# The second product of two feed-forwards: from plain products half by half to seven block products for both halves

## The chip, the cores and the metric

The kernel runs on one core of one Trainium2 chip. The metric is the device time of one execution in microseconds (us), as the median of several runs; a run with a profile leaves one execution in detail. Engines are named as in the profile: PE is TensorE (matmul), PEld its weight loads, DVE is VectorE, ACT is ScalarE, POOL is GpSimd, SP is SyncE, which here does nothing but issue all the DMAs, in one queue and in order.

## The reference

One layer of a trunk with 1,024 prompt tokens and 64 sample tokens (8 sequences of 8), a model width of 1,024 and a feed-forward width of 2,816, all in float32:

```python
def rmsnorm(x, g):
    y = x * lax.rsqrt(jnp.mean(x * x, axis=-1, keepdims=True) + EPS)
    return y * g

def swiglu(x, w_in, w_out):
    gu = x @ w_in                                  # 1024 -> 2 * 2816
    g, u = gu[..., :D_FF], gu[..., D_FF:]
    return (jax.nn.silu(g) * u) @ w_out            # 2816 -> 1024

x = x + 0.5 * swiglu(rmsnorm(x, norm_ffn1), ffn1_w_in, ffn1_w_out)
x = x + token_mixing(rmsnorm(x, norm_mix), ...)    # projections, pooling, convolution, scan, gates
x = x + 0.5 * swiglu(rmsnorm(x, norm_ffn2), ffn2_w_in, ffn2_w_out)
y = rmsnorm(x, norm_final)
```

The change lies in `(silu(g) * u) @ w_out`, the second product of each of the two feed-forwards, and in what stands next to it.

## The kernel before

**Tokens.** They lie in two halves: h0 has 512 (all prompt), h1 has 576 (512 prompt, 64 sample). Activations are kept transposed, features on the 128 partitions and tokens along the row, so a tile of h1 is 128x576. The width of 1,024 makes 8 blocks of rows (m or k), the feed-forward width 22 (ff).

**Products in float32.** An operand is split into a rounded part and the rest of it (names `hh` and `hr`, `wh` and `wl`, `hi` and `lo`, or both in one tile, `hl` and `hp`): ACT writes the rounded part, DVE subtracts it (`split`, L356 and L358; for weights L295 and L296 in `load_w`). A block product is then three matmuls: rounded by rounded, rounded weight by the rest, rest of the weight by rounded. All matmuls have one line, L164, and all transposes L168; they are told apart by the tile they write (`po` is the second product's).

**The stages.** Feed-forward 1, the projections into the token mixing (`in_proj`), the mixing, feed-forward 2, the final norm. In a feed-forward the first product is already done by seven block products instead of eight (`wino`, `ffn_in`), one ff after the other, with sums of weight blocks on GpSimd (L438) and parts of its exits on GpSimd too (L554, L575, L605). The gated hidden tile `g` of one ff and half goes to DRAM: `dma(hdram[h][ff], g)`.

**The second product before** (`ffn`, from L665 on) runs half by half. For a half all 22 hidden tiles are loaded (`hr<-hd`) and split; then for each of the 8 blocks of output rows, over 22 blocks of the inner dimension, `products` issues three matmuls of 512 columns for h0, or three times two matmuls of 288 columns for h1. That is 528 matmuls of 512 columns and 1,056 of 288 in each feed-forward. The weights of output blocks 0 and 1 were split ahead and wait in DRAM (`part`, `out01`); those of the others are loaded raw and split at the place. Each block leaves through DVE (L697: half the product plus the old x, which is reloaded from `xspill`).

**Order.** The program is written with generators ("chains") that are advanced at every step of a product (`tick()`), due at times of a count of matmul time: `start(gen, delay)` sets one going, `finish` runs it to its end. A scheduler then fixes an order for each engine, and every engine works through its own list in order. After feed-forward 1, `after1` starts the norm of the next stage as such a chain: for h0 it runs 25 us of that count into h1's second product (`HN_AT`), its normalised tiles go through DRAM (`xnd`) and come back. h1's norm follows h1's last block. In feed-forward 2 `half2` and `after2` do the same with the final norm, whose first part (`final_head`, output rows 0 to 3) and second part (`final`) transpose x and write the result.

## Time and profile before

| | before |
|---|---|
| runs | 2918.49 us median of 3 (2917.91 to 2923.22) |
| profiled execution | 2918.88 us, its span 2917.1 us |
| mean granted PE clock | 0.988 |
| PE, DVE, ACT, POOL busy | 97%, 58%, 47%, 34% |
| second product of feed-forward 1 | 523.4 to 788.7 us |
| second product of feed-forward 2 | 2633.9 to 2903.0 us |

The span is what the profile's records cover. The profile is one execution; "busy" of PE counts matmuls whose ends are modelled, and since matmuls are pipelined, the time of one in a group's row (from its start to its result) is longer than the distance between two. In a group's row stand line, engine, operation, tile written and tile read, the count, then the busy time in us, the mean of one in ns, and the idle time of the engine just before it with what ended it.

### The profile page before, as it was taken

How to read it: one execution, taken by the hardware profiler on the slowest of the kernel's cores; microseconds unless marked ns; L12 is line 12 of the kernel's file. 1: busy time of each engine (PE TensorE's matmuls, PEld its weight loads, DVE VectorE, ACT ScalarE, POOL GpSimd, SP SyncE). 2: the span in 40 equal slices, each digit the busy share in tenths (PEclk: the TensorE clock that was granted, in tenths of full speed). 3: DMA queues.
4: the chain of work that ended last, by engine and by line, in shares of the span. 5: the costliest groups of instructions: out<-in, count | busy, mean ns of one | idle time of the engine just before them, and what ended most of it. 6: DMA issues, size and time to landing. Idle time of an engine off the chain costs nothing. (4 is left out here: it accounts for less than half of the span.)

```text
span 2917.1 us, 52535 instructions
## 1 busy us (share of the span) xinstructions
PE 2828.8 (97%) x19306; PEld 2614.7 (90%) x19306; DVE 1706.4 (58%) x2702; ACT 1364.7 (47%) x3004; POOL 999.3 (34%) x1088
## 2 busy tenths in 40 slices
PE   7999999999999999999989999899999999999998
PEld 6999999889989999999988887678999999997898
DVE  6665555434483586766757776765665544453422
ACT  5444444323354555554556566566234444442322
POOL 6444444000132456464712343322134444440000
PEclk9999999999999999999999999998999999999999
DMA  4575554856445555634375678775764522236642
GB/s 134 168 226 183 162 173 130 283 185 194 115 129 164 163 188 162 201 107 128 104 263 182 198 230 247 251 252 171 251 230 144 163 92 82 78 118 200 218 156 73
DMA packets 520802, 502.84 MB, mean 172 GB/s; under 512 B 36564, under 2 KB 365128, under 8 KB 520536
## 3 DMA queue, kind: packets, MB, share of 16 engines
q1 hardware_dynamic: 520528, 499.47, 54.0%
q8 instruction: 152, 2.49, 0.4%
q14 instruction: 106, 0.87, 0.1%
q10 hardware_dynamic: 16, 0.00, 0.0%
HBM read 356.53 MB, written 143.05 MB: 171 GB/s over the span
## 5 line engine op out<-in xcount | busy, mean ns | idle before, releaser
L164 PE MATMUL pw<-X,wh 128*128 128x288 f32 (+2 forms) x2832 | 626.7, 310 | 3.8 <-ACT v L561 3.6
L164 PEld LDWEIGHTS pw<-X,wh 128*128 128x128 f32 x2832 | 461.7, 189 | 25.7 <-ACT v L561 4.2
L164 PE MATMUL pw<-X,wl 128*128 128x288 f32 (+1 forms) x1644 | 473.6, 288 | 0.6 <-DVE wl L445 0.6
L164 PE MATMUL pw<-hl,wh 128*128 128x256 f32 (+1 forms) x1536 | 393.1, 329 | 0.0
L445 DVE TENSOR_TENSOR wl<-s,wh 128x512 fp32r<-128x512 f32 x288 | 227.2, 790 | 238.3 <-ACT wh L444 216.4
L164 PE MATMUL pw<-hi,wh 128*128 128x288 f32 x1120 | 331.1, 296 | 1.1 <-ACT t L597 1.1
L164 PE MATMUL pw<-hi,wl 128*128 128x288 f32 x1120 | 329.8, 294 | 0.0
L164 PE MATMUL pw<-lo,wh 128*128 128x288 f32 x1120 | 329.7, 294 | 0.0
L438 POOL TENSOR_TENSOR s<-wraw,wraw 128x512 f32<-128x512 f32 x144 | 195.8, 1360 | 357.5 <-DVE wl L445 253.9
L164 PEld LDWEIGHTS pw<-X,wl 128*128 128x128 f32 x1644 | 311.7, 190 | 0.8 <-DVE wl L445 0.8
L164 PE MATMUL pw<-hl,wl 128*128 128x256 f32 x1072 | 300.7, 281 | 0.0
L296 DVE TENSOR_TENSOR wl<-wraw,wh 128x512 fp32r<-128x512 f32 x208 | 151.3, 729 | 246.6 <-ACT wh L295 241.5
L164 PEld LDWEIGHTS pw<-hl,wh 128*128 128x128 f32 x1536 | 259.8, 190 | 20.9
L295 ACT ACTIVATE wh<-wraw 128x512 fp32r<-128x512 f32 x208 | 125.6, 605 | 310.8 <-PE po L164 213.7
L444 ACT ACTIVATE wh<-s 128x512 fp32r<-128x512 f32 x288 | 181.1, 630 | 162.6 <-PE pw L164 138.3
L445 DVE TENSOR_TENSOR wl<-wraw,wh 128x512 fp32r<-128x512 f32 x216 | 168.7, 781 | 135.3 <-ACT wh L444 124.7
L164 PEld LDWEIGHTS pw<-hi,wh 128*128 128x128 f32 x1120 | 210.5, 188 | 7.8 <-ACT t L597 1.6
L164 PE MATMUL po<-hh,wh 128*128 128x288 f32 (+1 forms) x800 | 211.2, 324 | 4.4 <-ACT hh L356 3.5
L164 PE MATMUL po<-hr,wh 128*128 128x288 f32 (+1 forms) x800 | 211.6, 323 | 0.1
L164 PE MATMUL po<-hh,wl 128*128 128x288 f32 (+1 forms) x800 | 210.9, 323 | 0.0
L164 PEld LDWEIGHTS pw<-lo,wh 128*128 128x128 f32 x1120 | 210.6, 188 | 0.0
L164 PEld LDWEIGHTS pw<-hi,wl 128*128 128x128 f32 x1120 | 210.1, 188 | 0.0
(380 smaller groups left out, 6252.7 us busy)
## 6 DMA issues: line engine op xcount, KB each, us to landing
wraw<-in_ffn_w_in_dram SPq DMA_DIRECT2D x188, 256.0 KB
wh<-part SPq DMA_DIRECT2D x156, 256.0 KB
wl<-part SPq DMA_DIRECT2D x156, 256.0 KB
wraw<-in_w_in_dram SPq DMA_DIRECT2D x144, 256.0 KB
wraw<-in_ffn_w_out_dram SPq DMA_DIRECT2D x120, 256.0 KB
part<-ph SPq DMA_DIRECT2D x80, 256.0 KB
part<-pr SPq DMA_DIRECT2D x80, 256.0 KB
ab<-acsd SPq DMA_DIRECT2D x64, 256.0 KB
```

Source lines behind the costliest of these rows:

```text
L164: T.matmul(out, lhsT, rhs, start=start, stop=stop, skip_group_check=free)
L295: S.activation(wh, raw, AF.Copy)
L296: V.tensor_tensor(wl, raw, wh.bitcast(F32), op=ALU.subtract)
L438: G.tensor_tensor(t, a, b, op=op)
L444: S.activation(wh, a, AF.Copy)
L445: V.tensor_tensor(wl, a, wh.bitcast(F32), op=ALU.subtract)
```

## The change

The second product of both feed-forwards becomes `second`: 7 block products in place of 8 over a 2x2x2 cut (ff tiles even and odd; output rows 0 to 3 and 4 to 7; the first and second half of each token half), in the order 1, 2, 5, 6, 4, 7, 3. Each product runs over 4 output blocks and 11 pairs of ff tiles, with three matmuls of 256 columns (h0) and three of 288 (h1) beside each other on the same weights: 7 x 4 x 11 x 3 = 924 pairs in each feed-forward.

Its operands on the token side are seven sets of 11 tiles of 128x544, made in the first product's stage and put to DRAM (`hblock`): three are quarters of the hidden tiles (products 1, 2, 3), four are sums that GpSimd makes in place by a chain (`sums`, four subtractions for each half and pair of ff tiles). On the weight side nothing is split ahead any more: products 1, 2 and 4 take one raw weight block, 5, 6 and 7 a sum of GpSimd's, 3 what `fourth` left during product 4. Results are combined at the exits (`leave`). The last product is done for both halves on output rows 0 and 1, then for h0 on rows 2 and 3, then for h1, so that h0 ends 66 matmuls of 288 columns ahead of h1. h0's norm no longer runs beside h1's second product, and the round trip through `xnd` is gone; a part of the sum of squares is made ahead (`half1`), as are half of the stores of x.

```diff
-    def rstd(tiles, h, count, out, pace=1.0):
+    def rstd(tiles, h, count, out, pace=1.0, s=None):
...
-                dma(hdram[0][ff], g[:, : 2 * n])
+                hidden(0, ff, g)
...
-        for h in HALVES:
-            N = NTOK[h]
-            parts = [], []
-            for k in range(NFF):
...
-                dma(t, hdram[h][k])
-                split(t, a[:, :N], t.bitcast(F32R))
...
-            for ms in ((0, 1),) + tuple((m,) for m in range(2, KD)):
...
-                        wh, wl = load_w(wo, kb, n4, m * P)
-                        for kk in range(n4):
-                            products([pts], wh, wl, kk, slice(0, P), [(h, *parts)], kb + kk, NFF)
...
-            after(h, xt)
+        while hsums:
+            finish(hsums.pop(0))
+        second(wo, after, half)
...
+    def hidden(h, ff, g):
...
+        if ff % 2 == 0:
+            even[h] = g
+            put("1", g[:, f])
+            return
+        e = even[h]
+        put("2", g[:, f])
+        put("3", g[:, s_])
+
+        def sums():
+            for p, out, a, b in (("5", e[:, s_], e[:, s_], e[:, f]), ("6", g[:, s_], g[:, s_], e[:, s_]),
+                                 ("7", e[:, f], g[:, s_], e[:, f]), ("4", g[:, f], g[:, f], g[:, s_])):
+                G.tensor_tensor(out, a, b, op=ALU.subtract)
+                put(p, out)
+                yield H_PACE
+
+        hsums.append(start(sums(), H_AT))
...
+        def load_X(p):
...
+            dma(r, hblock[p][k])
+            split(r, a, r.bitcast(F32R))
...
+        def unit(p, m, hs, ws):
+            pts = [psum("pd", "po" + p)[:, : NPAIR[h]] for h in hs]
+            for kb, nk, wh, wl in ws:
+                for kk in range(nk):
...
+                    for j, (W_, lo_) in enumerate(((wh, 0), (wh, 1), (wl, 0))):
+                        for h, pt in zip(hs, pts):
...
+                            mm(pt, W_[:, kk, :], X[p][k][lo_][:, at : at + NPAIR[h]],
...
+            for h, pt in zip(hs, pts):
+                leave(p, m, h, pt)
...
+            for m in range(4):
...
+                unit(p, m, HALVES, weights(p, m))
+                if p == "4":
+                    fourth(m)
+                for _ in range((0, 3, 3, 2)[m]):
+                    load_X(nxt)
+        for h in HALVES:
+            half(h, xt[h])
+        for m in (0, 1):
+            unit("3", m, HALVES, weights("3", m))
...
+        for h in HALVES:
+            for m in (2, 3):
+                unit("3", m, [h], kept[m] if h else keep(m))
+            after(h, xt[h])
...
     def after1(h, xt):
         o = []
-        if h == 0:
-            prep1m[0] = start(norm_parts(xt, 0, i_gm, o, HN_PACE, xnd), HN_AT), o
-        for m in range(KD):
+        s, c = ssq1[h]
+        finish(c)
+        prep1m[h] = start(norm_parts(xt, h, i_gm, o, (0.5, 1.2)[h], s), 0.0), o
+        for m in range(4):
             dma(xspill[h][m], xt[m][:, : NTOK[h]])
-        if h == 1:
-            finish(prep1m[0][0])
...
-            for k in (0, 4, 1, 5, 2, 6, 3, 7):
-                dma(xn[k][:, : NTOK[0]], xnd[k])
...
-    ffn(wi1, ffn1_w_out[0], prep1, after1, side=side())
+    ffn(wi1, ffn1_w_out[0], prep1, after1, half1, side())
```

Three places of the order that the change gives, each before and after. In the rows stand the line, the operation, the tile written and the tiles read with their numbers, the shape, and in brackets the engines and queues whose signals the instruction waits for.

PE where feed-forward 1 ends and `in_proj` begins, before: `po` is the second product, `pdt` the first result of the projections, and `hl` are the normalised tiles of h0, one number for each of the 8 blocks.

```order
L164 MATMUL po_8616<-hh_7331,wl_8769 128x288
L164 MATMUL pdt_8813<-hl_7838,wh_8815 128x512 [waits Activation_49]
L164 MATMUL pdt_8813<-hl_7838,wh_8815 128x512
L164 MATMUL pdt_8813<-hl_7838,wl_8816 128x512 [waits DVE_49]
L164 MATMUL pdt_8813<-hl_7868,wh_8815 128x512 x2
L164 MATMUL pdt_8813<-hl_7868,wl_8816 128x512
L164 MATMUL pdt_8813<-hl_7904,wh_8815 128x512 x2
```

The same place after; `pg` is the result of the gates' projection.

```order
L165 MATMUL po_1646_9454<-hh_9102,wl_9382 128x288
L165 MATMUL pdt_9540<-hl_9501,wh_9542 128x512 [waits Activation_49]
L165 MATMUL pg_1681_9605<-hl_9501,wh_9607 128x512
L165 MATMUL pdt_9540<-hl_9501,wh_9542 128x512 [waits DVE_49]
L165 MATMUL pdt_9540<-hl_9501,wl_9543 128x512
L165 MATMUL pdt_9540<-hl_9506,wh_9542 128x512 [waits Activation_49]
L165 MATMUL pg_1681_9605<-hl_9501,wh_9607 128x512
L165 MATMUL pg_1681_9605<-hl_9501,wl_9608 128x512
L165 MATMUL pg_1681_9605<-hl_9506,wh_9607 128x512
L165 MATMUL pdt_9540<-hl_9506,wh_9542 128x512 [waits DVE_49]
```

Before, `pdt` waited for the weights' two parts alone, and the tiles `hl` stood ready; now each block's `hl` is itself waited for, its rounded part from ACT and its rest from DVE, and the gates' matmuls are put between.

DVE around h0's norm, before: `xn` is the normalised tile, `hl` its rest, `wl` the rest of a weight tile of h1's second product, `x` an exit of it.

```order
L393 TENSOR_SCALAR rsm_7761<-pss_7756 128x4 [waits PE_49]
L296 TENSOR_TENSOR wl_7857<-wraw_7855,wh_7856 128x256 [waits DMAHW2_49,PE_49,Activation_49]
L799 SCALAR_TENSOR_TENSOR xn_7837<-x_6575,cols,r_7800 128x512 [waits Activation_49]
L296 TENSOR_TENSOR wl_7887<-wraw_7885,wh_7886 128x512 [waits DMAHW3_49,PE_49,Activation_49]
L358 TENSOR_TENSOR hl_7838<-xn_7837,hl_7838 128x512 [waits Activation_49]
L799 SCALAR_TENSOR_TENSOR xn_7867<-x_6578,cols,r_7800 128x512 [waits DMAHW3_49,DVE_49]
L296 TENSOR_TENSOR wl_7923<-wraw_7921,wh_7922 128x512 [waits DMAHW4_49,PE_49,Activation_49]
L358 TENSOR_TENSOR hl_7868<-xn_7867,hl_7868 128x512 [waits Activation_49]
L697 SCALAR_TENSOR_TENSOR x_7879<-po_7682,x_7879 128x288 [waits PE_49]
```

The same after; L795 is an exit of the last product, L946 what was L799.

```order
L397 TENSOR_SCALAR rsm_9447<-pss_9442 128x4 [waits PE_49]
L795 SCALAR_TENSOR_TENSOR x_7148<-po_1639_9399,x_7148 128x288 [waits PE_49]
L296 TENSOR_TENSOR wl_9608<-wraw_9606,wh_9607 128x512 [waits DMAHW1_49,Activation_49]
L946 SCALAR_TENSOR_TENSOR xn_9500<-x_6954,cols,r_9479 128x512 [waits Activation_49]
L795 SCALAR_TENSOR_TENSOR x_7252<-po_1646_9454,x_7252 128x288 [waits PE_49,Pool_49]
L946 SCALAR_TENSOR_TENSOR xn_9505<-x_7044,cols,r_9479 128x512
L358 TENSOR_TENSOR hl_9501<-xn_9500,hl_9501 128x512 [waits Activation_49]
L946 SCALAR_TENSOR_TENSOR xn_9510<-x_7146,cols,r_9479 128x512
L358 TENSOR_TENSOR hl_9506<-xn_9505,hl_9506 128x512 [waits Activation_49]
L946 SCALAR_TENSOR_TENSOR xn_9515<-x_7250,cols,r_9479 128x512
```

Before, the norm's steps were spread between the weights of h1's long second product; now the first of them stands just ahead of the last exit of the whole second product (`x_7252`), and the others follow it.

POOL in the first product's stage of feed-forward 1, before, one ff: L438 are sums of weight blocks for the next ff, the others the exits.

```order
L438 TENSOR_TENSOR s_741_3939<-wraw_3869,wraw_3871 128x512 [waits DMAHW1_49,DMAHW0_49,DVE_49]
L438 TENSOR_TENSOR s_742_3941<-s_741_3939,wraw_3865 128x512 [waits DMAHW5_49,DVE_49,Pool_49]
L554 TENSOR_TENSOR g_3639<-g_3639 128x256 [waits DVE_49]
L438 TENSOR_TENSOR s_754_4004<-wraw_3865,wraw_3869 128x512 [waits DVE_49]
L438 TENSOR_TENSOR s_758_4035<-wraw_3867,s_742_3941 128x512 [waits DMAHW4_49,DVE_49,Pool_49]
L554 TENSOR_TENSOR t_3640<-t_3640 128x256 [waits DMAHW2_49,DVE_49]
L554 TENSOR_TENSOR g_3639<-v_3641 128x256 [waits DVE_49,Pool_49]
```

A piece of the same stage after, in which one pair's sums stand (L702):

```order
L579 TENSOR_TENSOR g_4757<-g_4757,t_4758 128x256 [waits Activation_49]
L609 TENSOR_TENSOR g_4775<-g_4775,t_4774 128x288 [waits Activation_49]
L702 TENSOR_TENSOR g_4757<-g_4757,g_4503 128x256 [waits DMAHW3_49,Pool_49]
L702 TENSOR_TENSOR g_4503<-g_4757,g_4503 128x256 [waits DMAHW4_49,Pool_49]
L442 TENSOR_TENSOR s_941_5270<-wraw_5202,wraw_5204 128x512 [waits DMAHW2_49,DMAHW1_49,DVE_49]
L702 TENSOR_TENSOR g_4775<-g_4775,g_4521 128x288 [waits DMAHW5_49]
L702 TENSOR_TENSOR g_4757<-g_4757 128x256 [waits DMAHW6_49]
L702 TENSOR_TENSOR g_4521<-g_4775,g_4521 128x288 [waits Pool_49]
L702 TENSOR_TENSOR g_4775<-g_4775 128x288 [waits DMAHW0_49]
L442 TENSOR_TENSOR s_942_5272<-s_941_5270,wraw_5198 128x512 [waits DVE_49]
```

The subtractions stand in POOL's list between the exits and the weight sums, and most of them wait for a DMA queue: they write over a tile that a put to DRAM is still to have read.

200 lines of the change are left out of this document (151 added, 49 removed).

## The prediction

> **What bounds the kernel now.** First the page: how busy each engine is.
>
> ```profile
> span 2917.1 us, 52535 instructions
> PE 2828.8 (97%) x19306; PEld 2614.7 (90%) x19306; DVE 1706.4 (58%) x2702; ACT 1364.7 (47%) x3004; POOL 999.3 (34%) x1088
> ```
>
> PE carries the kernel; the others have room on average. Whether that holds where the change sits I read from busy times by stretch: the first product's stage of feed-forward 1, the end of it, its second product, the first 31 us of the projections, then the same places of feed-forward 2 and the tail. Columns: stretch, its length, busy PE, PEld, DVE, ACT, POOL with counts, granted PE clock, DMA share, GB/s.
>
> ```profile
> 146.00:438.00 292.00, 290.88 (x1957) 273.08 (x1956) 168.91 (x279) 138.29 (x304) 129.87 (x123) 1.00 0.58 186
> 511.00:523.00 12.00, 12.00 (x88) 11.60 (x87) 12.00 (x22) 11.04 (x24) 2.28 (x2) 1.00 0.88 298
> 523.40:788.70 265.30, 263.79 (x1599) 240.42 (x1598) 103.26 (x163) 78.46 (x133) 8.68 (x11) 1.00 0.61 193
> 788.70:820.00 31.30, 30.83 (x143) 24.63 (x141) 24.33 (x45) 16.72 (x33) 13.41 (x16) 1.00 0.37 102
> 2620.00:2634.00 14.00, 13.82 (x86) 11.68 (x84) 12.44 (x22) 9.94 (x21) 1.49 (x3) 1.00 0.90 313
> 2633.90:2903.00 269.10, 266.36 (x1635) 244.66 (x1634) 87.83 (x144) 72.77 (x133) 1.02 (x1) 0.99 0.49 156
> 2634.00:2640.00 6.00, 3.26 (x9) 2.36 (x8) 2.08 (x3) 1.89 (x3) 0.00 (x0) 0.72 0.89 302
> 2640.00:2650.00 10.00, 10.00 (x45) 8.24 (x45) 2.08 (x3) 1.90 (x3) 0.00 (x0) 1.00 0.85 278
> 2903.00:2917.00 14.00, 0.95 (x7) 0.45 (x5) 5.77 (x13) 4.81 (x12) 1.17 (x1) 0.62 0.48 169
> ```
>
> Both second products are full of matmuls (263.8 of 265.3 us, 266.4 of 269.1), with DVE, ACT and POOL mostly idle. So matmul time taken out there comes off the span, as far as the feed keeps up. The seam into the projections, 788.7 to 820, has half a microsecond of idle PE: h0's norm was hidden. DMA reaches 313 GB/s at 0.90 of its time, the best these rows show, against 193 and 156 in the second products.
>
> The chain of work that ended last gives the distance of matmuls where nothing else intervenes (start, length, what, count), and the groups by form give the time of one.
>
> ```profile
> 2630.87 5.46 DMA hr<-hd
> 2637.03 59.77 PE po L164 x255
> ...
> 2836.70 64.78 PE po L164 x486
> ```
>
> ```profile
> L164 PE MATMUL po<-hr,wh 128*128 128x288 f32 x576 | 123.3, 296 | 0.0
> L164 PE MATMUL po<-hr,wh 128*128 128x512 f32 x224 | 88.3, 395 | 0.1
> L164 PE MATMUL pw<-hl,wl 128*128 128x256 f32 x1072 | 300.7, 281 | 0.0
> ```
>
> **The matmuls.** 512 columns: 59.77 / 255 = 234 ns. 288 columns: 64.78 / 486 = 133 ns. That is 101 ns for 224 columns, 0.45 ns each, so 256 columns should cost 133 - 32 x 0.45 = 119 ns; the groups' times fall in step (395, 296, 281). Before, a feed-forward had 528 x 234.4 + 1,056 x 133.3 = 264.5 us, which is what the stretch shows. After: 924 pairs of (119 + 133.3) = 233.1 us. Gain 31.4 us for each feed-forward, **62.8 us** for both.
>
> **What that costs at the start.** The new first product needs operand tiles that SP loads behind the last puts of the stage ahead, which wait for the last gates; the second half's last sums follow. The way is a DMA, a split on ACT and one on DVE:
>
> ```profile
> L356 ACT ACTIVATE hh<-hr 128x576 fp32r<-128x576 f32 x36 | 24.7, 685 | 61.9 <-DMA hr<-hd 59.7 <-PE ptf L168 2.1
> L358 DVE TENSOR_TENSOR hr<-hr,hh 128x576 fp32r<-128x576 f32 x36 | 27.3, 758 | 55.8 <-ACT hh L356 55.6
> ```
>
> 5.46 + 0.69 + 0.76 = 6.9 us, against some 19 to 37 matmuls (2.4 to 4.7 us) that stand ahead on PE: 2 to 4.5 us, and with the slowed clock (below) I take 4. Before, feed-forward 1 lost nothing here (PE 12.00 of 12 us) and feed-forward 2 lost 6.00 - 3.26 = 2.7 us. So +4 and +1: **5 us** (0 to 11).
>
> That half-speed clock is in the rows: the wait near 2634 leaves 0.72 granted over six microseconds and 1.00 after them. The Trainium skill (TensorE: Matmul & The Clock Gate, HAM oscillation) says that only PE pauses above about 3.4 us cost clock; by that rule a 2.7 us pause costs nothing further. This trace disagrees, since the stretch that holds the pause is slowed beyond it. By the row I count 1 us of slowed clock in each start's 4; by the page the sum of losses would be 2 us lower.
>
> **Between the products.** Each product's tiles are loaded during the one before, so that they have the DMA's 6.9 us; only the second product's last tiles, 38 to 68 matmuls ahead of their use (5 to 9 us), are close: 1.5 us. At the change from 2 to 5 a weight rest stands on DVE behind an exit, which waits for the last matmul:
>
> ```profile
> L697 DVE SCALAR_TENSOR_TENSOR x<-po,x 128x288 f32<-128x288 f32 x32 | 13.1, 452 | 12.4 <-PE po L164 12.4
> L296 DVE TENSOR_TENSOR wl<-wraw,wh 128x512 fp32r<-128x512 f32 x208 | 151.3, 729 | 246.6 <-ACT wh L295 241.5
> ```
>
> 0.45 + 0.73 = 1.2 us. DVE otherwise has slack: 64 exits, 84 weight rests and 77 tiles, 64 x 0.45 + 84 x 0.73 + 77 x 0.76 = 149 of 233 us. Then the feed. In product 7 a block of output rows needs two raw weights, 1.44 MB, three operand tiles, 0.8 MB, and four of old x, 1.1 MB: 13 MB in its 33.3 us; product 4 needs 9 MB. Together 22 MB in 66.6 us, 330 GB/s against the 313 seen: 70 us, or 79 at the 278 of the row at 2640. The weights stand some 130 matmuls ahead of their use in the order, 16 us, and that takes up most: 1.5 us (0 to 12.5). Sum of this part 4.2 for each feed-forward, **8 us** (2 to 31).
>
> **The seam into the projections.** Before, h0's norm ran beside h1's 141 us (1,056 x 133.3 ns). Now h0 ends only 66 matmuls, 8.8 us, ahead. The steps of the norm, h0's (512 columns) and h1's:
>
> ```profile
> L381 DVE TENSOR_TENSOR ssq<-ssq,sq 128x576 f32<-128x576 f32 x7 | 6.7, 961 | 1.4 <-ACT sq L380 1.3
> L799 DVE SCALAR_TENSOR_TENSOR xn<-x,cols,r 128x512 f32<-128x512 f32 x8 | 6.0, 750 | 6.9 <-DMA xnd<-xn 4.9 <-ACT r L402 2.0
> L358 DVE TENSOR_TENSOR hl<-xn,hl 128x512 fp32r<-128x512 f32 x8 | 5.5, 691 | 3.0 <-ACT hl L356 2.8
> L402 ACT COPY r<-prb 128x512 f32<-128x512 f32 x2 | 1.2, 587 | 2.8 <-PE prb L168 2.8
> L364 POOL TENSOR_TENSOR rsm<-rsm,mhalf 128x5 f32<-128x5 f32 x1 | 1.2, 1167 | 5.1 <-DVE rsm L395 5.1
> ```
>
> The transposes of the reciprocal root (`prb`) stand on PE after 53 of the 66 matmuls, at 7.1 us; with them and the copy r is there at some 8.5 us. Eight pairs of 0.75 + 0.69, with the hand-over to ACT about 1.6 us, end at 21.3. h1's sum of squares follows on DVE, 4 x 0.96, to 25.1, and PE, in order, waits there for it. From 8.8 to 25.1 PE has 24 matmuls of `pdt` and 17 of the gates, 41 x 0.234 = 9.6 us. Idle: 16.3 - 9.6 = 6.7 us, and 0.9 more at POOL's power (1.17, under three matmuls). After that the block sums for the projections wait behind the 11.5 us that the eight pairs add to DVE, which had 24.3 of 31.3 us already: 36 us of DVE against 31 of PE. I take 3.4 for that and 1 for the clock: **12 us** (6 to 20).
>
> **The tail.** h0's final transposes now share 8.8 us with h1's matmuls, and more output is written in the 14 us after the last matmul: **1.5 us** (-1 to 5).
>
> **The first product's stage.** POOL gets 8 subtractions for each of 11 pairs of ff, four of 256 and four of 288 columns:
>
> ```profile
> L554 POOL TENSOR_TENSOR g<-g 128x256 f32<-128x256 f32 x38 | 29.4, 773 | 0.1
> L605 POOL TENSOR_TENSOR g<-g,t 128x288 f32<-128x288 f32 x40 | 43.3, 1082 | 23.8 <-ACT g L602 20.1
> ```
>
> 4 x 0.77 + 4 x 1.08 = 7.4 us for a pair, which takes PE about 42 us (168 matmuls for an ff, 126 ns each). POOL's share was 129.87 / 292 = 44%, 18.7 us; now 26 of 42. What hides it:
>
> ```profile
> POOL s L438 <- DVE wl L445: 277.2, 128, 11.9
> ```
>
> The weight sums wait for free buffers (277 us in all), so they run ahead and can be put off. SP gets 308 small puts for 88 whole ones, and loses the split weights' traffic. For waits on puts I take **2 us** (0 to 30).
>
> **Sum.** 62.8 - 5 - 8 - 12 - 1.5 - 2 = 34.3 us. The profiled execution took 2918.88 us, 1.8 above its span and 0.4 above the median of 2918.49; I subtract from the median: **2884 us**.
>
> **The rivals.**
> *Slower: POOL's in-order list in the first product's stage.* Most of the eight subtractions wait for a put to have read the tile. With 26 of 42 us busy POOL has 16 us for such waits in each pair; a wait costs up to the 5.46 us of the DMA row, behind it stand the next exits and weight sums, and PE waits for those. The gain is gone once 22 pairs lose 1.6 us each, that is at 17.6 us of waits, 3.2 full waits a pair. Four full waits: 22 x (21.8 - 16) = 128 us, 3012 us. For it: DMA is at 0.58 in that stage and puts stand behind loads. Against: the sums start 4 us after the puts, and waits of one pair overlap. 11%.
> *The feed binds.* At 278 GB/s products 4 and 7 cost 12.5 us in both feed-forwards, of which 1.5 are counted: 22 us less gain, 2906 us. For it the rows above; against it the lead. 15%.
> *The seam is light.* If PE finds other matmuls and DVE keeps up, it costs 3 us, and if nothing is lost between the products: 9 + 8 us more gain, 2867 us. 14%.
> *Narrow matmuls cost more than their columns.* If a weight load set the pace, 256 columns would take 133 ns, a pair 266.6, and a feed-forward 246.3: 26 us less gain, 2910 us. Against it: 281 ns beside 296. The Trainium skill (TensorE: Matmul & The Clock Gate, Back-to-back issue gap) gives 81 ns for 128 columns and 131 for 512 in a stream with weight loads, by which halving the columns loses; the trace disagrees, 133 ns at 288 and 234 at 512. 4%.
> That the matmuls do not fall to 924 pairs is excluded by the loops.
>
> **How the numbers follow.** The forecast has 56%, its own range 2866 to 2905 (seam 6 to 20, start and feed to half their bounds). The rivals have 14% at 2867, 15% at 2906, 4% at 2910, 11% at 3012. No change that a measurement can tell is within 0.2%, 2912.7 to 2924.3: 5%, from the upper edges of the feed and narrow cases. Slower is POOL's case and a remnant of the feed: 12%. Faster: 83%. The range from 2862 to 2914 leaves out the slow case and a little at each end.
>
> **What would show it.** Right: matmuls of `po` at 119 and 133 ns, second products of about 240 us each, PE idle some 7 to 12 us between the last `po` and the first projections with DVE's norm named, POOL near 60% in the first product's stage with PE still full there. Wrong: PE idle in the first product's stage with POOL or a put named (slower), DMA above 0.9 with `wl` or `hp` late in products 4 and 7 (feed), or no idle time at the seam.

## The result, and the profile after

The changed kernel takes **2995.66 us** (median of 4 runs, 2992.67 to 2997.95), the kernel before 2918.2 us beside it (median of 4, 2912.97 to 2923.22): **1.0265 times the time [1.0245, 1.0285]**. It is slower by 77 us; 34 us less were forecast, with a range that ended at 2914.

The page of the kernel after, engine by engine:

```profile
span 2990.9 us, 54693 instructions
PE 2813.4 (94%) x19834; PEld 2624.2 (88%) x19834; DVE 1859.9 (62%) x2848; ACT 1400.5 (47%) x3086; POOL 1345.7 (45%) x1392
```

PE's busy time fell by 15 us only, though 63 us of matmul work went away, and its share fell from 97% to 94%. Where the rest is, the busy times by stretch tell. First the kernel before, in three stages that the prediction did not show whole: first product of feed-forward 1, the seam with the first part of the projections, first product of feed-forward 2. Columns as there: stretch, length, busy PE, PEld, DVE, ACT, POOL, granted PE clock, DMA share, GB/s.

```profile
101.40:523.50 422.10, 418.96 (x2814) 393.45 (x2813) 248.58 (x408) 205.08 (x448) 188.22 (x176) 1.00 0.56 179
788.70:865.60 76.90, 74.76 (x442) 66.14 (x441) 63.13 (x110) 39.59 (x86) 32.88 (x35) 1.00 0.44 124
2217.00:2628.80 411.80, 410.04 (x2746) 385.79 (x2745) 217.50 (x345) 184.14 (x386) 186.67 (x178) 1.00 0.35 112
```

The same view of the kernel after: first product 1, second product 1, seam, first product 2, second product 2 with its last transposes.

```profile
110.60:559.80 449.20, 425.95 (x2814) 397.89 (x2813) 253.85 (x395) 196.91 (x434) 259.38 (x254) 0.98 0.53 166
559.80:832.00 272.20, 246.75 (x1862) 240.75 (x1860) 162.43 (x231) 98.24 (x175) 96.87 (x70) 0.96 0.67 203
832.00:927.00 95.00, 82.41 (x442) 69.24 (x442) 79.24 (x130) 46.33 (x100) 44.84 (x42) 0.93 0.35 97
2281.00:2699.30 418.30, 411.76 (x2747) 386.33 (x2746) 227.32 (x332) 176.42 (x372) 252.21 (x256) 1.00 0.35 108
2699.30:2975.50 276.20, 252.31 (x1904) 246.39 (x1903) 163.35 (x234) 99.92 (x189) 97.86 (x70) 0.96 0.59 179
```

Each row is read in two steps: length less PE busy is idle time; PE busy at equal work grows where the clock is below 1, and by up to 0.2 us at each pause, since a matmul is counted to its end (295 ns in the groups of `po`) where the next would have begun after some 126. First product 1: 23.3 us idle instead of 3.1, and 7 us more for the same 2,814 matmuls. Seam: 12.6 us idle instead of 2.1, and 7.7 us more busy time at a mean clock of 0.93. Both second products: 25 and 24 us idle, where before there were 1.5 and 2.7.

The ends of a stage are taken in the table at the first matmul on a named tile, those of the second products at the last on `po`. "Opening" is all that stands ahead of the first `pw`.

| us | opening | first product 1 | second product 1 | seam | mixing | first product 2 | second product 2 |
|---|---|---|---|---|---|---|---|
| before | 101.4 | 422.1 | 265.1 | 77.0 | 654.6 | 411.8 | 272.3 |
| after | 110.6 | 449.3 | 271.9 | 95.2 | 657.3 | 418.2 | 275.8 |
| difference | +9.2 | +27.2 | +6.8 | +18.2 | +2.6 | +6.4 | +3.5 |

With -0.1 for the rest these make the 73.8 us between the two spans (2990.9 and 2917.1).

Who ended the idle time of PE in the second products shows in the view of the tile `po`, kernel after:

```profile
  ACT wh L745: 44.9, 18
  DVE wl L746: 33.9, 38
  ACT hh L356: 22.6, 18
  PE po L165: 15.6, 11
  DVE hr L358: 3.9, 10
```

These sums count weight loads and matmuls both, so only their order is used: the splits of weights (`wh`, `wl`) stand first, those of the operand tiles (`hh`, `hr`) second.

### The profile page after: what moved, and what is told of

The parts are those of the page before. It is cut to its first block, busy times and chain, and to the rows that moved or that the text cites. A ratio compares the mean times of both kernels' runs of the same rounds, so it can differ in the third digit from the quotient of the medians.

```text
span 2990.9 us, 54693 instructions
## 1 busy us (share of the span) xinstructions
PE 2813.4 (94%) x19834; PEld 2624.2 (88%) x19834; DVE 1859.9 (62%) x2848; ACT 1400.5 (47%) x3086; POOL 1345.7 (45%) x1392
## 5 line engine op out<-in xcount | busy, mean ns | idle before, releaser
L449 DVE TENSOR_TENSOR wl<-s,wh 128x512 fp32r<-128x512 f32 x288 | 252.3, 876 | 282.0 <-ACT wh L448 260.9
L449 DVE TENSOR_TENSOR wl<-wraw,wh 128x512 fp32r<-128x512 f32 x216 | 174.9, 811 | 110.6 <-ACT wh L448 101.5
L165 PE MATMUL po<-hh,wh 128*128 128x256 f32 (+1 forms) x848 | 186.3, 296 | 20.2 <-ACT hh L356 10.2
L165 PEld LDWEIGHTS pw<-hl,wl 128*128 128x128 f32 x1072 | 203.0, 189 | 0.0
L448 ACT ACTIVATE wh<-wraw 128x512 fp32r<-128x512 f32 x216 | 135.5, 627 | 141.0 <-PE pw L165 121.5
L165 PE MATMUL po<-hh,wl 128*128 128x256 f32 (+1 forms) x848 | 185.4, 295 | 7.3 <-DVE wl L746 7.0
L165 PE MATMUL po<-hr,wh 128*128 128x256 f32 (+1 forms) x848 | 185.0, 295 | 1.1 <-DVE hr L358 1.0
```

The lines of the kernel that those rows point to most:

```text
L165: T.matmul(out, lhsT, rhs, start=start, stop=stop, skip_group_check=free)
L448: S.activation(wh, a, AF.Copy)
L449: V.tensor_tensor(wl, a, wh.bitcast(F32), op=ALU.subtract)
```

## The experiments

Each is one edit on the kernel after, unless another is named. The table gives medians, the ratio to the kernel before with its 95% interval, and from one profiled execution the excess of each stage over the kernel before, in us (op: opening, f1, f2: first products, s1, s2: second products). Second products that were not touched came out between 271.1 and 280.8 (s1) and 275.3 and 281.3 (s2), so a few us in one of these columns mean nothing. The profiled execution of e9_turn (3010 us) is the longest of its five.

| kernel | median | ratio | op | f1 | s1 | seam | f2 | s2 |
|---|---|---|---|---|---|---|---|---|
| after | 2995.66 | 1.0265 [1.0245, 1.0285] | +9.2 | +27.2 | +6.8 | +18.2 | +6.4 | +3.5 |
| e3_nosub | 2958.47 | 1.0140 [1.0125, 1.0155] | +2.9 | +3.1 | +11.3 | +18.0 | +1.2 | +4.4 |
| e5_dvesub | 2986.78 | 1.0239 [1.0221, 1.0257] | +2.5 | +12.6 | +15.7 | +17.9 | +7.9 | +6.3 |
| e6_gpq | 3046.77 | 1.0447 [1.0427, 1.0468] | +13.1 | +53.5 | +6.0 | +17.9 | +31.2 | +4.3 |
| e7_aside | 2974.61 | 1.0202 [1.0183, 1.0222] | +6.3 | +15.9 | +6.9 | +18.0 | +1.4 | +4.4 |
| e9_turn | 2995.19 | 1.0257 [1.0236, 1.0277] | +7.3 | +26.9 | +14.1 | +18.4 | +9.1 | +9.0 |
| e11_silu | 2987.68 | 1.0240 [1.0225, 1.0255] | +7.4 | +24.7 | +8.8 | +18.4 | +0.4 | +3.0 |
| e15_stage1 | 2975.46 | 1.0189 [1.0171, 1.0206] | +5.1 | +13.9 | +6.8 | +18.4 | +6.4 | +3.5 |
| e2_xodve | 2985.31 | 1.0223 [1.0197, 1.0248] | +11.0 | +28.0 | +3.5 | +17.8 | +4.8 | -3.3 |
| e8_start | 2990.27 | 1.0250 [1.0230, 1.0270] | +9.0 | +28.7 | +12.0 | +17.9 | +8.9 | -1.1 |
| e10_oneraw | 2974.37 | 1.0197 [1.0180, 1.0213] | +9.8 | +29.1 | -3.8 | +18.0 | +8.9 | -6.5 |
| e16_nox | 2918.57 | 1.0001 [0.9992, 1.0011] | +9.4 | +27.3 | -32.5 | +17.9 | +8.6 | -34.0 |
| e17_noxoneraw | 2916.78 | 0.9997 [0.9986, 1.0008] | +8.9 | +27.5 | -31.9 | +18.0 | +6.9 | -34.6 |
| e19_nodma | 2947.85 | 1.0096 [1.0076, 1.0116] | +11.3 | +25.1 | -15.3 | +17.8 | +7.3 | -15.3 |
| e20_nosplit | 2943.03 | 1.0085 [1.0066, 1.0103] | +10.1 | +27.5 | -18.3 | +18.0 | +6.7 | -23.3 |
| e12_seam | 2994.58 | 1.0261 [1.0248, 1.0275] | +14.3 | +23.8 | +11.6 | +7.4 | +6.2 | +10.9 |
| e13_all | 2968.43 | 1.0171 [1.0158, 1.0184] | +11.1 | +22.3 | +2.5 | +7.4 | +0.3 | -1.1 |
| e14_ffn2 | 2915.47 | 0.9991 [0.9982, 1.0000] | +1.0 | +1.1 | +0.6 | 0.0 | +0.4 | -8.5 |
| e18_best | 2949.91 | 1.0106 [1.0091, 1.0121] | +8.1 | +11.1 | +5.3 | +7.5 | +7.8 | -8.7 |

### The first product's stage: sums or puts?

**No sums** (e3_nosub):

```diff
-                G.tensor_tensor(out, a, b, op=ALU.subtract)
                 put(p, out)
```

> Edit: the four subtractions for each pair and half in the first product's stage are left out, the puts stay (products 5, 6, 7 and 4 then run on plain quarters, so part of the computation is left out). Theory A, SP's queue stands at puts that wait for POOL: the puts find their tiles ready, the stages go back to before, 36 + 6 us less: about 2955. Theory B, POOL's own time in its in-order list: the same. Rival C, the 308 small puts themselves (SP's issue time and DMA traffic): 2990 to 2996.

Opening and first product 1 lose 6 us instead of 36, first product 2 loses 1 instead of 6. With the sums gone the same puts cost next to nothing. How a sum on GpSimd reaches PE can be seen in two places of the kernel after. First the timeline of POOL over one burst of sums (start, length, engine, line, operation):

```profile
338.33 1.10 POOL L609 TENSOR_TENSOR g<-g,t 128x288 f32<-128x288 f32 x1
340.08 2.11 POOL L702 TENSOR_TENSOR g<-g,g 128x256 f32<-128x256 f32 x2 [0.65 <-DMA hb<-g]
342.14 1.30 POOL L442 TENSOR_TENSOR s<-wraw,wraw 128x512 f32<-128x512 f32 x1
343.40 1.26 POOL L702 TENSOR_TENSOR g<-g,g 128x288 f32<-128x288 f32 x1
...
346.84 1.27 POOL L442 TENSOR_TENSOR s<-s,wraw 128x512 f32<-128x512 f32 x1
348.08 0.72 POOL L558 TENSOR_TENSOR g<-g 128x256 f32<-128x256 f32 x1
```

Six of the pair's eight sums stand in this burst, 5.7 us, with two weight sums of 2.6 us among them; the other two came behind the ff before. The exit's addition (L558) of the next ff stands behind the whole burst in POOL's list and starts nearly 9 us after the last exit step of the ff before (L609) has ended. ACT's SiLU needs it, and ACT was idle for 5.62 us until it came. That wait, over both feed-forwards, in the groups by form of ACT: before, after, and without the sums.

```profile
L559 ACT ACTIVATE g<-g 128x256 f32<-128x256 f32 x38 | 15.9, 418 | 83.9 <-POOL g L554 83.9
```

```profile
L563 ACT ACTIVATE g<-g 128x256 f32<-128x256 f32 x38 | 15.9, 418 | 151.6 <-POOL g L558 151.6
```

```profile
L563 ACT ACTIVATE g<-g 128x256 f32<-128x256 f32 x38 | 15.9, 418 | 96.8 <-POOL g L558 96.8
```

Second, the timeline of SP's queue in the kernel after:

```profile
145.21 0.80 SPq L689 DMA_DIRECT2D hb<-g  x2
...
146.63 8.01 SPq L689 DMA_DIRECT2D hb<-g  x7
...
155.66 0.44 SPq L926 DMA_DIRECT2D xin<-in_x_prompt_dram  x1
```

and of PE:

```profile
159.89 1.12 PE L169 MATMUL ptr<-ident,xin 128*128 128x128 f32 x4 [5.23 <-DMA xin<-in_x_prompt_dram]
```

Seven puts take 8 us where two took 0.8 just before. 4.6 us of that are waits for GpSimd's sums, the longest 2.9, by the waits of SP. The load of x (`xin`) stands behind them, for the transposes that put x aside until the end of the feed-forward (`turn_x`), and PE, in order, stops at those transposes. In the waits of PE in first product 1 of the kernel after, these loads have 13.5 of the 23.3 idle us:

```profile
PE ptr L169 <- DMA xin<-in_x_sample_dram: 8.3, 2, 4.2
PE ptr L169 <- DMA xin<-in_x_prompt_dram: 5.2, 1, 5.2
```

In the kernel before, the same view of the same stage has no wait for x.

**The sums on DVE** (e5_dvesub) and **the sums into a tile of their own** (e7_aside):

```diff
-                G.tensor_tensor(out, a, b, op=ALU.subtract)
+                V.tensor_tensor(out, a, b, op=ALU.subtract)          # e5_dvesub
```

```diff
+            aside = act((P, 576), name="sc")
-                G.tensor_tensor(out, a, b, op=ALU.subtract)
+                G.tensor_tensor(aside[:, :n], a, b, op=ALU.subtract) # e7_aside
```

> Edit: the same subtractions on DVE instead of POOL, 176 of some 0.4 us. Theory A: the puts wait less long, 10 to 30 us less, 2965 to 2985. Theory B: POOL is as before the change, 25 to 40 us less, 2955 to 2970, unless DVE's list now holds the rests of the weights up. C: no change.

> Edit: POOL makes the same 176 sums, but into a tile that nobody reads; the puts carry the plain quarters (part of the computation is left out). POOL's work is all there, but neither SP waits for a sum nor a sum for a put. Theory A, the two queues hold each other up (SP at puts, POOL at landed puts): head and first product's stages fall back as without sums, from 36 + 6 us over before to 6 + 1, about 2958. Theory B, POOL's own time ahead of exits and weight sums: they stay at 30 to 40 over before, 2985 to 2996.

The rows of first product 1 in e3_nosub, e7_aside and e5_dvesub, from the busy times by stretch of each:

```profile
104.30:529.60 425.30, 418.59 (x2815) 392.24 (x2814) 237.93 (x393) 198.62 (x433) 185.62 (x175) 1.00 0.55 175
```

```profile
107.70:545.70 438.00, 425.23 (x2814) 397.57 (x2813) 255.14 (x393) 194.93 (x432) 258.77 (x254) 0.98 0.54 170
```

```profile
103.90:538.70 434.80, 423.24 (x2815) 396.50 (x2814) 274.26 (x471) 196.36 (x432) 187.18 (x175) 0.99 0.54 171
```

In e7_aside GpSimd does the same 259 us of work, but no sum waits for a put to have read its tile, and no put for a sum. That returns 14 of the 36 us in feed-forward 1 and 5 of the 6 in feed-forward 2. Of the 22 that stay in feed-forward 1, 6 stay without any sum too (e3_nosub); 16 are for GpSimd's time itself. On DVE the sums cost 15 us in feed-forward 1 and 8 in the other; the whole run does not separate from the kernel after, since its second product 1, which the edit leaves alone, came out 9 us longer (that of e9_turn 7 us). So neither half of the mechanism is all of it: of the 30 us that go with the sums in feed-forward 1, the coupling through tiles is about half, GpSimd's time the rest.

That rest can reach PE in two ways that no run separates: by what stands behind the burst in POOL's list, and by DVE, which works slower beside it. From 110 to 520 us a weight's rest (`wl<-s,wh`, 128x512) took 903 ns in the kernel after and 899 in e7_aside, but 776 without the sums and 777 with the sums on DVE.

**The puts of the sums issued by GpSimd** (e6_gpq):

```diff
-                put(p, out)
+                nc.gpsimd.dma_start(hblock[p][i][:, at : at + n], out)
```

> Edit: the puts of the four sums are issued from POOL's own queue, right behind the subtraction; SP's queue keeps the three plain quarters. Theory A: SP no longer waits for POOL, 25 to 40 us less, 2955 to 2970. Theory B: POOL has even more to do (176 issues), no gain or slower, 2990 to 3020.

This frees SP's queue, and is worse by 50 us. In its groups by form of POOL:

```profile
L703 POOL DMA_DIRECT2D hb<-g x176 | 98.6, 561 | 29.9 <-POOL g L702 26.1 <-issue 2.9 <-DMA wraw<-in_ffn_w_in_dram 0.3
```

0.56 us of its list for each issue, 98.6 us in all, on the engine whose list was already late.

**Two covers taken away one by one, then together.** e9_turn puts the transposes of x further behind their loads, e11_silu puts the exit's addition ahead of SiLU on DVE, e15_stage1 does both and gives the first pair's sums to DVE:

```diff
-                yield 4.0
+                yield 10.0                                              # e9_turn, in turn_x
```

```diff
-                halves(g[:, f], g)
+                V.tensor_tensor(g[:, f], g[:, f], g[:, s_], op=ALU.add) # e11_silu, in after0
```

```diff
-                G.tensor_tensor(out, a, b, op=ALU.subtract)             # e15_stage1, with both above
+                (V if i == 0 else G).tensor_tensor(out, a, b, op=ALU.subtract)
```

> Edit: in feed-forward 1 the transposes of x stand 10 instead of 4 us of matmul time behind their loads. Theory A in the narrow sense: the three pauses of 4 to 5.4 us at these transposes go, with the clock after them, 14 to 22 us less, 2972 to 2982. Theory B: the time returns elsewhere in the stage, less than 5 us gained.

> Edit: one addition per ff and feed-forward (the sum ahead of the first SiLU of h0 in the first product's exits, 38 in all) goes from POOL to DVE. Theory B1: POOL's sums stand in its list ahead of this addition, ACT waits for it at the SiLU (151.6 us in all against 83.9 before), and PSUM exits and weight parts stand behind on ACT: the stages go back most of the way, 15 to 30 us less, 2965 to 2980. Theory A, SP's queue standing at the puts, is what counts: less than 6 us, 2989 to 2996.

> Edits in feed-forward 1's first product alone: those of e11_silu and e9_turn together, and the four sums of the first pair of ff on DVE (the head). If both POOL's list (at ACT's SiLU) and SP's list (at x's transposes) cover each other, the two edits that gained 8 and 0 us alone gain 20 to 28 together: head and stage from 36 over before to 8 to 16 over, about 2965. If the stage is held by POOL's time itself: no more than 10 us less, 2985.

e9_turn gives some 2 us in feed-forward 1. e11_silu gives 4 us in opening and first product 1, and the 6 of first product 2; neither run separates from the kernel after by its interval. Together with the first pair on DVE they give 17 in feed-forward 1. The waits of PE say why e9_turn gave so little: in first product 1 it waits no longer for x (13.5 us in the kernel after), but its other waits there, for exits on DVE and ACT, grow from 9.4 to 22.4 us. So the two waits cover each other, and taking the load of x away leaves PE to the exits. What the first pair gives by itself wasn't tried.

These two edits of e15_stage1 on sums and exits stand in code that both feed-forwards use. In first product 2 the 6 us that e11_silu returns are lost again: PE stands 3.9 us in one piece for a weight's rest of DVE, 5.0 in e18_best, which has the same edits. DVE has the first pair's sums there, and they are the likely cause; e11_silu and e13_all, without them, have no such wait.

### The second products: matmuls, loads or splits?

**Old x added on DVE** (e2_xodve) and **one raw weight for each sum** (e10_oneraw, on e2_xodve):

```diff
-                    G.tensor_tensor(xt[h][q][:, : 2 * n], xt[h][q][:, : 2 * n], o, op=ALU.add)
+                    V.tensor_tensor(xt[h][q][:, : 2 * n], xt[h][q][:, : 2 * n], o, op=ALU.add)
```

```diff
-                    x, y = raw(0, 1, m, kb, nk), raw(1, 1, m, kb, nk)
+                    x = raw(0, 1, m, kb, nk)
-                        G.tensor_tensor(a, x, y, op=ALU.add)
+                        G.tensor_tensor(a, x, x, op=ALU.add)            # product 5; product 7 likewise
```

> Edit: in product 7 the 16 additions of the old x (32 in both feed-forwards) are done by DVE instead of POOL. Theory F1, POOL's in-order list: the weight sums of product 7 stand behind additions that wait for exits, and PE waits for them (pauses of 4.7, 1.9 and less late in each second product, about 9 us with the slowed clock). Then 12 to 18 us go in both: about 2980. Rival F2, the six buffers for raw weights and the DMA's 4 to 5 us set the pace: no more than 3 us, 2992 to 2996.

> Edit on top of e2_xodve (2985 us; its second products 268.6 and 269.0 us): products 5 and 7 load one raw weight instead of two and POOL adds it to itself (part of the computation is left out), 12 MB in place of 18 for these two's weights. Theory F2, the raw weights' buffers and DMA set the pace: 6 to 12 us less in each second product, about 2965 to 2972. Theory F1, POOL's list: no more than 3 us.

e2_xodve shortens the second products by 3 and 7 us, little more than the scatter, e10_oneraw by another 7 and 3. Both together leave them 28 us above the bare matmuls (below). So half of the raw weights of products 5 and 7 is a small part of the loss.

**No operand tiles but the first product's** (e16_nox, on e2_xodve: products 2 to 7 multiply the tiles of product 1), and **with one raw weight on top** (e17_noxoneraw):

```diff
+            if p != "1":
+                X[p].append(X["1"][k])
+                return
...
-            elif p == "1":
-                a, r = fx(F32R, "hh"), fx(name="hr")
```

> Edit on top of e2_xodve: all seven products run on the operand tiles of product 1, so 66 of 77 tile loads and their splits on ACT and DVE go (part of the computation is left out). Second products of 268.6 and 269.0 us there. Theory F3, the tiles' loads stand in SP's queue and their rests on DVE ahead of the weights': 244 to 250. Theory F2, the six raw buffers: 260 or more.

> Edits of e16_nox and e10_oneraw together (parts of the computation are left out). If tiles and raw weights are all that keeps the second product from its matmuls' 233 us: 238 to 244 with the start. If POOL, the exits or the clock hold it too: 250 or more.

The second products of e16_nox by stretch:

```profile
560.20:792.80 232.60, 232.57 (x1861) 232.35 (x1860) 109.79 (x181) 62.03 (x109) 68.37 (x54) 1.00 0.54 159
2663.90:2902.20 238.30, 237.78 (x1901) 236.82 (x1901) 109.64 (x186) 63.68 (x123) 67.02 (x54) 1.00 0.45 131
```

PE is full to 0.03 us at a clock of 1.00, and 232.6 us is the 233.1 worked out in the prediction from 119 and 133 ns. So all the loss that e2_xodve leaves in the second products comes with the 66 operand tiles of products 2 to 7, and the weights alone keep up: e17_noxoneraw, with fewer of them, gains nothing more (233.2 and 237.7).

A tile is a DMA and two splits. **Splits without DMA** (e19_nodma) and **DMA without splits** (e20_nosplit), both on e2_xodve:

```diff
-            dma(r, hblock[p][k])
-            split(r, a, r.bitcast(F32R))
+            if p == "1":
+                dma(r, hblock[p][k])
+                split(r, a, r.bitcast(F32R))
+            else:
+                split(X[order[order.index(p) - 1]][k][1].bitcast(F32), a, r.bitcast(F32R))   # e19_nodma
```

```diff
+            if p != "1":
+                r = act((P, 576), name="hr")[:, :N2]
+                dma(r, hblock[p][k])
+                X[p].append(X["1"][k])
+                return                                                                      # e20_nosplit
...
-            elif p == "1":
-                a, r = fx(F32R, "hh"), fx(name="hr")
```

> Edit on top of e2_xodve: the 66 later operand tiles are still split by ACT and DVE into buffers of their own, but from the tile of the product before, not from a load (part of the computation is left out). Second products of 268.6 and 269.0 us there, 232.6 and 238.3 without tiles. If DVE's and ACT's lists (the rests ahead of the weights') hold the product: 255 or more. If DMA and SP's queue do: 245 or less.

> The opposite edit on top of e2_xodve: the 66 tiles are loaded (18 MB in each feed-forward), but neither split nor used. If DMA's rate and SP's issues hold the product: 255 or more. If the splits on ACT and DVE, and the buffers that PE frees late, do: 245 or less.

Second product 1 by stretch in e2_xodve, e19_nodma and e20_nosplit:

```profile
562.60:831.20 268.60, 246.86 (x1861) 242.07 (x1860) 165.05 (x248) 99.42 (x175) 71.63 (x54) 0.96 0.68 206
```

```profile
559.90:809.70 249.80, 238.86 (x1861) 236.24 (x1860) 162.59 (x250) 101.39 (x179) 73.97 (x54) 0.98 0.51 151
```

```profile
561.20:808.00 246.80, 237.01 (x1861) 235.86 (x1860) 107.31 (x181) 61.65 (x109) 67.05 (x54) 0.98 0.74 224
```

Against e16_nox the splits alone cost 17 and 19 us, the DMAs alone 14 and 11; both together 36 and 31. Each run came out between the two values expected of it: both count, the splits a little more, and they nearly add up. In neither run does a split wait for a late load, or a matmul for a late-loaded tile, in products 2 to 7 (in e20_nosplit nothing reads the tiles). What this cannot tell is whether a DMA costs by its bytes or by its place in SP's queue, since the DMA of e20_nosplit has both.

**The tiles of the start earlier** (e8_start):

```diff
-            if k >= 4:
+            if k < 7 if p == "1" else k >= 4:
```

> Edit: of product 1's operand tiles it is the last four, not the first four, that take the late-freed buffers, so the tiles needed first are loaded first. If the start of the second product (pauses of 4 to 5 us and the slowed clock behind them) is set by the order of these loads in SP's queue: 4 to 7 us less in each feed-forward, about 2984. If it is set by the last gates: no change, 2992 to 2996.

It does not separate from the kernel after. The start itself is in the stretches of the kernel after,

```profile
559.80:575.00 15.20, 11.74 (x68) 10.47 (x67) 7.30 (x12) 5.79 (x11) 4.14 (x4) 0.78 0.78 242
2699.30:2715.00 15.70, 12.15 (x70) 10.88 (x69) 8.77 (x13) 6.68 (x13) 3.69 (x4) 0.78 0.84 267
```

and those of e16_nox:

```profile
559.80:575.00 15.20, 15.17 (x121) 14.95 (x121) 7.26 (x11) 5.45 (x12) 3.67 (x4) 1.00 0.67 197
2663.90:2680.00 16.10, 15.85 (x125) 15.50 (x125) 6.71 (x12) 5.70 (x11) 3.18 (x4) 1.00 0.60 177
```

68 matmuls instead of 121 in 15.2 us, at 126 ns each 6.7 us lost, about half of them as idle time and half by the clock of 0.78. In feed-forward 2 they are 70 in 15.7 us instead of some 122, 6.5 us lost. e16_nox loads the same eleven tiles of product 1 and starts without a loss; but besides having no tiles of product 2 to load, it holds those of product 1 in other buffers, so which of the two frees the start is open.

### The seam

**The last product half by half from the first output row on** (e12_seam), so that h0 ends 132 matmuls ahead of h1 instead of 66:

```diff
-        for m in (0, 1):
+        for m in ():
...
-            for w in weights("3", m, own=m == 3):
+            for w in weights("3", m, own=m >= 1):
-            for m in (2, 3):
+            for m in (0, 1, 2, 3):
```

> Edit: the last product is done for h0 on all four output blocks and then for h1 on all four (the weights' parts are kept), so h0 ends 132 instead of 66 matmuls ahead. If the seam's 18 us are h0's norm lacking cover: 6 to 9 us less, about 2987. If they are DVE's load there: no more than 2 us less.

The seam of e12_seam by stretch:

```profile
837.00:921.40 84.40, 78.32 (x443) 67.37 (x442) 71.47 (x121) 42.08 (x92) 39.81 (x39) 0.98 0.38 108
```

6.1 us idle instead of 12.6, and a clock of 0.98: 10.8 us won back. The second products take 5 and 7.5 us more in this run, the first of them within the scatter, and the whole run does not separate from the kernel after; it was expected to be 6 to 9 us faster.

### All together, and one feed-forward alone

**e13_all** is e2, e8, e11 and e12; **e18_best** is e2, e8 and e15, with e12 in feed-forward 1 alone; **e14_ffn2** leaves feed-forward 1 and its seam as before, and takes feed-forward 2 with e2, e8 and e11:

```diff
+        if half is None:                                      # e14_ffn2: feed-forward 1
+            for h in HALVES:                                  # the loop of before
...
+        if not mode[0]:
+            dma(hdram[h][ff], g[:, : NTOK[h]])
+            return
...
-    ffn(wi1, ffn1_w_out[0], prep1, after1, half1, side())
+    ffn(wi1, ffn1_w_out[0], prep1, after1, side=side())
```

> Edits of e2_xodve, e8_start, e11_silu and e12_seam together. If their causes are independent the gains add up: 10 + 5 + 15 to 30 + 6 to 9 us, 2942 to 2960. If the stages lose by POOL's and SP's lists as such and each edit only moves a wait: 2970 or more.

> All edits that left the result whole: e2_xodve, e8_start, e15_stage1, and e12_seam in feed-forward 1 alone. Worked out by stage from their runs: head and first stage 10 to 16 over before, second product 1 about 2 over, seam 7 over, second product 2 about 8 under: 2928 to 2936, still slower than before; below 2918 only if the edits' gains multiply.

> Feed-forward 1 and the seam as before the change, feed-forward 2 with seven products and the edits of e2_xodve, e8_start and e11_silu. Before, the changed stages of feed-forward 2 took 412 and 272 us; if the edits bring 412 to 414 and 262 to 268 us: 2908 to 2915, faster than before. If the seam and the first product's stage of feed-forward 1 were not where the loss is: 2925 or more.

Second product 2 of e14_ffn2 by stretch:

```profile
2634.20:2898.00 263.80, 245.82 (x1900) 241.18 (x1900) 164.64 (x250) 100.35 (x189) 74.04 (x54) 0.98 0.62 188
```

With all edits the change still costs 31 us, of which the seam and first product 1 with its opening have 27; 2928 to 2936 us were expected of e18_best, so the edits' gains did not add up. In feed-forward 2 alone, which has no seam behind it and no x to load ahead, it gives 8.5 us in its stage and 0.9991 [0.9982, 1.0000] over 12 runs: no more than level with the kernel before.

## Why the prediction was wrong

**The matmuls: right.** 62.8 us forecast, 32.5 + 34.0 measured when the tiles are free (e16_nox). The rival of narrow matmuls (4%) is out: a pair takes 232.6 / 924 = 252 ns.

**The start: too small.** 5 us forecast (0 to 11). By the rows above 6.7 and 6.5 us are lost, and before, feed-forward 2 had lost 2.7 there: 10.5 in place of 5, near the end of the range given.

**Between the products: this step failed.** 4.2 us for each feed-forward (up to 15). Measured: 271.9 - 232.6 = 39 us and 275.8 - 238.3 = 37.5, less 6.7 and 6.5 for the start: **33 and 31**. Two sentences of the step did not hold. "They have the DMA's 6.9 us" takes the duration of a DMA and its splits once it is issued; in SP's queue, in order, it stood behind loads of weights that wait for a buffer, and itself waited for PE to free one. From the waits of SP in second product 1, kernel after (total, times, longest):

```profile
SPq L736 <- DVE wl L746: 44.9, 24, 3.9
...
SPq L729 <- PE po L165: 19.4, 15, 13.0
```

L736 loads weights, L729 operand tiles. And "DVE otherwise has slack", 149 of 233 us, compares an average: it was 162 of 272 in the end, and yet e20_nosplit, which takes 66 splits from ACT and DVE, gives 22 us. The longest pause of second product 1, 4.56 us from 752.3 on, shows one way from a late tile to PE, in the timelines of POOL, SP and ACT:

```profile
747.56 1.02 POOL L766 TENSOR_TENSOR ws<-wraw,wraw 128x384 f32<-128x384 f32 x1 [1.63 <-DMA wraw<-in_ffn_w_out_dram]
750.10 0.48 SPq L729 DMA_DIRECT2D hp<-hb  x1
755.74 0.66 ACT L356 ACTIVATE hp<-hp 128x544 fp32r<-128x544 f32 x1 [9.15 <-DMA hp<-hb]
756.30 1.03 ACT L745 ACTIVATE wh<-ws 128x384 fp32r<-128x384 f32 x2
```

The weight's sum that PE needs next is ready at 748.6. Its split stands in ACT's list behind the split of an operand tile, and that tile is loaded only from 750.1 on, behind twelve loads of weights that SP took 13.5 us to issue. ACT stands idle for 9.15 us, and PE with it from 752.3. How much of the loss goes this way isn't shown: e19_nodma and e20_nosplit, in which no split waits for a late load, together have 31 of the 36 us of e2_xodve in this stage.

The rival "the feed binds" named the right neighbourhood, with 11 us for each feed-forward and a ceiling of 313 GB/s. At this pause 313 was no ceiling: the tile took 5.6 us from its issue to ACT, about the 5.46 of the DMA in the prediction, and in the 6.8 us from 755.0 on the kernel moved 393 GB/s. Whether bytes cost elsewhere stays open, as e20_nosplit cannot tell; the rival's sign, DMA above 0.9, does stand in the row of this pause.

In the rows the loss of second product 1 is 25 us idle and 14 us more busy time for the same matmuls (246.75 against 232.57). The idle time is 16 pauses of 0.4 to 4.6 us, by count in the timeline. Of the 14 us the clock has 8.4: it was at 0.50 in four stretches, in which PE was busy for 16.8 us, and at 1.00 in the rest of the stage.

```profile
563.90:570.70 6.80, 5.44 (x20) 4.61 (x21) 3.37 (x4) 2.40 (x4) 2.92 (x3) 0.50 0.53 171
639.00:642.30 3.30, 3.26 (x14) 3.26 (x15) 3.30 (x5) 0.92 (x2) 2.53 (x2) 0.50 0.60 151
755.00:761.80 6.80, 4.70 (x19) 4.38 (x20) 2.74 (x6) 2.43 (x5) 0.07 (x1) 0.50 1.05 393
802.80:806.20 3.40, 3.40 (x17) 3.40 (x16) 3.19 (x6) 3.40 (x8) 0.00 (x0) 0.50 0.02 5
```

These follow the four longest pauses, of 2.53, 4.25, 4.56 and 3.13 us; behind the twelve others, up to 1.75 us, no new one begins. The pause of 4.56 us cost 2.4 us in clock, half of the 4.70 busy. The Trainium skill (TensorE: Matmul & The Clock Gate, HAM oscillation) has pauses beyond about 3.4 us slow the clock; the pauses of 4.25 and 4.56 us agree, those of 2.53 and 3.13 us do not, as the prediction read it off the wait of 2.7 us. Of the other 5.8 us the 16 pauses as such have 2.7, an estimate: each counts a matmul to its end, 0.295 - 0.126 us. The rest stays open.

**The seam: the mechanism right, its size within the range.** 12 us forecast (6 to 20), 18.2 measured: 10.5 more idle and 7.7 more busy time, of which the clock has 5.1 (0.50 from 850.6 to 864.2, with PE busy for 10.21 us), where 1 had been taken. The waits named are those of the forecast: the longest is 3.64 us before the sum of squares of h1, on DVE. What was too small are DVE's prices, in the groups by form from 826 to 860 us:

```profile
L358 DVE TENSOR_TENSOR hl<-xn,hl 128x512 fp32r<-128x512 f32 x8 | 8.7, 1087 | 0.0
L946 DVE SCALAR_TENSOR_TENSOR xn<-x,cols,r 128x512 f32<-128x512 f32 x8 | 7.4, 922 | 2.9 <-ACT r L406 2.9
```

The eight pairs took 16.1 us of DVE where 0.75 and 0.69 make 11.5. GpSimd works beside them, on sums of the projections' operands: the first of these subtractions, before it begins, took 0.68 us, the last six, beside it, 1.21 to 1.23. e12_seam shows the cause of the seam's loss, by returning 10.8 of it.

**The tail: right.** 1.5 us forecast, -0.2 measured.

**The first product's stage: this step failed.** 2 us forecast (0 to 30); 36.4 measured in opening and first product 1, 6.4 in first product 2. What it said hides the sums did not hold: "can be put off" is so for the weight sums, but the exit's addition stands in the same list, behind six of a pair's eight sums, and SiLU behind it. And it took waits on puts as small, where a put that waits for GpSimd stops SP's queue: up to 3.9 us for one put and 8 us for a run of seven, with the load of x behind. Without the sums 6 us are left of the 36. The rival "POOL's in-order list" (11%, 3012 us) had the right engine and its sign, PE idle in this stage, came true; that the end came 16 us from its time is luck. It saw the loss as GpSimd waiting for puts, four waits or 21.8 us in each of 22 pairs, some 480 us; in the kernel after GpSimd waited 40 us for puts ahead of its sums, by the view of L702. e7_aside, which takes these waits and those of the puts for the sums away together, returns 14 and 5 us; the larger part is GpSimd's time itself.

**The sum by what was measured.** Gain 66.5; start and between 39.3 and 37.5; seam 18.2; first products with opening 36.4 and 6.4; mixing 2.6; tail and rest -0.1: 140.3 - 66.5 = 73.8 us, the difference of the spans. No term that counts had the wrong sign; two of six, between the products and the first product's stage, were sized from averages, 10 us together where some 107 were lost (33, 31, 36.4 and 6.4), and took the forecast with them.

## What to carry to other kernels

Price work that is added to an engine "with room" by its place in that engine's list: ask what stands behind it, and give the burst's whole length to the shortest chain there (here 5.7 us of sums, and the weight sums between them, ahead of a 0.7 us addition). Price what runs beside it, too, at the time that it takes there, as DVE's subtractions below. The same holds for a queue of DMAs that is issued in order: a put that waits for a slow engine holds every load behind it, and no average share of the DMAs shows that. And when matmuls get fewer, every feed that was hidden gets less cover at the same time as it grows; a test with the feed taken out (e16_nox) and put back by parts tells in three runs what share each part has.

## What the runs showed of the hardware

DVE's subtraction for a split got slower by what GpSimd did beside it. The group by form and the view of the tile `hr` in the kernel after (in the second, the shortest, median and longest in ns):

```profile
L358 DVE TENSOR_TENSOR hr<-hr,hh 128x544 fp32r<-128x544 f32 x106 | 104.6, 988 | 83.0 <-ACT hh L356 82.7
```

```profile
L358 DVE TENSOR_TENSOR hr<-hr,hh x106: 706/725/1941, 283.4 to 2937.9; 128x544 fp32r<-128x544 f32 x106
```

The median is 0.73 us, the mean 0.99, the longest more than twice the median. Laid beside GpSimd's instructions in the same trace, all 154 subtractions of 128x544 part in two: 89 with next to no GpSimd work beside them have a median of 724 ns, 62 with GpSimd at work for 30% of their time or more one of 1434. The same group's mean was 908 ns in e2_xodve (GpSimd without the additions of old x) and 842 in e10_oneraw (its sums also from one raw block, and fewer loads); the kernel before, with GpSimd nearly idle in that stage, had 758 for 576 columns. The prediction priced the splits at 758. The Trainium skill (GPSIMD Engine Reference, Specifications) says that GpSimd shares its interfaces to SBUF with VectorE and that instructions with two inputs from SBUF contend; these rows agree, and the 30% of the mean, or twice the time for one subtraction, are a measure of it. And the DMAs moved 393 GB/s over 6.8 us, a quarter more than the 313 that the trace before had shown at its best.
